# A gradient along rows: tiles of 256 adjoining rows, or two of each partition's 64 rows

## The chip, the cores and the metric

The kernel runs on one core of one Trainium2 chip. The metric is device time in microseconds (us) of one execution, as the median of several runs; lower is better. A profile is one more execution, recorded by the hardware profiler, with a time of its own.

## The reference

```python
def setup_inputs():
    return {"x": np.random.randn(8192, 8192).astype(np.float32)}

def reference(x):
    return np.gradient(x, axis=1)
```

Along each row, an inner column gets half the difference of its two neighbours, (x[j+1] - x[j-1]) / 2. The first column gets x[1] - x[0] and the last one x[8191] - x[8190], both without the half. The matrix has 256 MiB, which are read once and written once: 536.87 MB (with 1 MB = 10^6 bytes).

## The kernel before

**Tiles.** A row has m = 8192 elements of 4 bytes, 32 KB. A tile takes R = 2 rows on each of the 128 partitions, so 256 rows, and there are nsets = 32 tiles. In the kernel before, tile s is the rows 256 s to 256 s + 255, and partition p holds the rows 256 s + 2 p and 256 s + 2 p + 1 of it: a piece of 64 KB that lies without a gap in DRAM, right behind the piece of partition p - 1. A tile is thus one run of 8.39 MB in DRAM. The output is cut in the same way.

**Buffers.** Three slots (NB = 3) of 64 + 16384 elements a partition rotate. A tile is loaded into the elements from 64 on, and its result is written from element 0 on, in the same slot. A small tile `ends` keeps four edge values a partition for each tile.

**One tile's work** (the loop over i):

- L52, on SyncE's DMA queue (SP): the load of the tile, one DMA of 8.39 MB.
- L74, on GpSimd (POOL): one small subtraction takes both rows' first and last differences into `ends`. It waits for the load.
- L80, on VectorE (DVE): one custom operation over both rows at once, 128 x 16382 elements, writes half the difference of the neighbours. It waits for L74, since it writes over what L74 reads.
- L91, on VectorE, or for some tiles on GpSimd: a copy of the four edge values to their places in the result. It waits for L80.
- L56, on SP: the store of the tile, one DMA of 8.39 MB. It waits for L91.

**The order of the transfers.** All loads and stores are issued by SP, in an order written out by hand: the loads of tiles 0, 1 and 2; then the tiles' stores as they get ready; behind the store of every third tile, the next three loads. A load waits until the store that used its slot three tiles before has landed. The store of a tile with i % 3 = 1 is held back until the next tile has landed (the variable `held`). So transfers go by threes: three loads, three stores, three loads, and so on.

The lines that decide where a tile lies in DRAM are L27 and L28; every load reads `x_sets[i]` and every store writes `out_sets[i]`.

Of the kernel before, what the change touches and what calls it, by code (L numbers as in the profile page):

```python
# [1 line left out]

# [4 lines left out]


@with_exitstack
def kernel(  # L10
    ctx: ExitStack,
    tc: tile.TileContext,
    x: bass.AP,
    out: bass.AP,
):

    nc = tc.nc
    P = nc.NUM_PARTITIONS
    n, m = x.shape
    R = 2  # L20
    NB = 3
    SH = 64
    W = R * m
    nsets = n // (P * R)
    f32 = x.dtype

    x_sets = x.rearrange("(s p t) m -> s p (t m)", p=P, t=R)  # L27
    out_sets = out.rearrange("(s p t) m -> s p (t m)", p=P, t=R)  # L28

    pool = ctx.enter_context(tc.tile_pool(name="pool", bufs=1))  # L30
    edge = 256 // 4
    nends = nsets * R * 2
    ends_pad = pool.tile([P, nends + edge // 2], f32, name="ends", tag="ends")
    ends = ends_pad[:, 0:nends].rearrange("p (s t e) -> p s t e", t=R, e=2)
    slots = [pool.tile([P, SH + W], f32, name=f"slot{k}", tag=f"slot{k}") for k in range(NB)]
    loads, stores = [], [None] * nsets
    in_front = {}

    def chain(i, ins, *needed):

        group, engine = f"slot{i % NB}", ins.ins.engine
        keep = [o.ins for o in needed]
        if in_front.get(engine, (None,))[0] == group:
            keep.append(in_front[engine][1])
        tc.declare_no_dep(ins.ins, group=group, keep=keep, reason="implied by the needed step")
        tc.add_to_no_dep_group(group, ins.ins)
        in_front[engine] = group, ins.ins
        return ins

    def load(i):  # L50
        b = slots[i % NB]
        ins = nc.sync.dma_start(out=b[:, SH : SH + W], in_=x_sets[i])  # L52
        loads.append(chain(i, ins, *([stores[i - NB]] if i >= NB else [])))

    def store(i, done, later):
        ins = nc.sync.dma_start(out=out_sets[i], in_=slots[i % NB][:, 0:W])  # L56
        stores[i] = chain(i, ins, done)
        if later is not None:
            tc.add_manual_dep(
                ins.ins,  # L60
                later.ins.name,
                mybir.DependencyInfo(mybir.DependencyClass.Sync, mybir.DependencyReason.DATA),
                reason="issued once the next tile has landed",
            )

    held = None
    with tc.manual_schedule():
        for i in range(NB):
            load(i)
        for i in range(nsets):  # L70
            b = slots[i % NB]
            xin = b[:, SH : SH + W].rearrange("p (t m) -> p t m", m=m)

            ins = nc.gpsimd.tensor_sub(  # L74
                out=ends[:, i, :, :],
                in0=xin[:, :, 1 : m : m - 2],
                in1=xin[:, :, 0 : m - 1 : m - 2],
            )
            at = [chain(i, ins, loads[i])]
            ins = nc.vector._custom_dve(  # L80
                dve_ops.TENSOR_TENSOR_REDUCE_SUB_MAX,
                out=b[:, 1 : W - 1],
                in0=b[:, SH + 2 : SH + W],
                in1=b[:, SH : SH + W - 2],
                s0=0.0,
                s1=0.5,
            )
            halved = chain(i, ins, *at)
            res = b[:, 0:W].rearrange("p (t m) -> p t m", m=m)
            placer = nc.gpsimd if i % 5 in (1, 3) and i < nsets - 2 else nc.vector  # L90
            ins = placer.tensor_copy(out=res[:, :, 0 : m : m - 1], in_=ends[:, i, :, :])  # L91
            placed = chain(i, ins, halved)
            if held is not None:
                store(*held, at[0])
                held = None
            if i % NB == 1 and i + 1 < nsets:
                held = i, placed
            else:
                store(i, placed, None)
            if i % NB == NB - 1:  # L100
                for k in range(i + 1, min(i + 1 + NB, nsets)):
                    load(k)


# [1 line left out]
_INS = ['x']  # L106
_OUTS = [((8192, 8192), 'float32')]


# [23 lines left out]
```

## Time and profile before

| | us |
|---|---|
| median of 3 runs | 1247.27 (1246.84 to 1247.35) |
| the profiled execution | 1246.62 |
| its span, from the first to the last instruction | 1244.7 |
| 32 L80 operations on VectorE, 17.22 each | 551.2 |
| 32 L74 operations on GpSimd, 0.198 each | 6.3 |
| 32 L91 copies, 20 on VectorE and 12 on GpSimd | 5.7 |
| issue to landing of a load, median | 57.9 |
| issue to landing of a store, median | 40.2 |

The page gives each engine's busy time, then the span in 40 equal slices of some 31 us, in which a digit is the busy share in tenths; the rows DMA and GB/s of the slices show how busy the core's 16 DMA engines were and what they moved, reads and writes together. Below that, DMA queues are listed with their packets (pieces that one DMA engine moves as one) and bytes, and groups of instructions with their count, busy time, the mean time of one in ns, and the idle time of their engine before them with what ended it. The trace also has a record of each DMA packet with its size, start and duration; it does not say which engine or partition a packet belongs to. The time from issue to landing counts the wait behind earlier transfers too. TensorE and ScalarE are not used.

### The profile page before, as it was taken

How to read it: one execution, taken by the hardware profiler on the slowest of the kernel's cores; microseconds unless marked ns; L12 is line 12 of the kernel's file. 1: busy time of each engine (PE TensorE's matmuls, PEld its weight loads, DVE VectorE, ACT ScalarE, POOL GpSimd, SP SyncE). 2: the span in 40 equal slices, each digit the busy share in tenths (PEclk: the TensorE clock that was granted, in tenths of full speed). 3: DMA queues.
4: the chain of work that ended last, by engine and by line, in shares of the span. 5: the costliest groups of instructions: out<-in, count | busy, mean ns of one | idle time of the engine just before them, and what ended most of it. 6: DMA issues, size and time to landing. Idle time of an engine off the chain costs nothing.

```text
span 1244.7 us, 237 instructions
## 1 busy us (share of the span) xinstructions
DVE 554.6 (45%) x52; POOL 8.8 (1%) x48
## 2 busy tenths in 40 slices
DVE  2850582079009702850582079009603840591082
POOL 0000000000000000000000000000000000000000
DMA  9999999999999999999999999999999999999999
GB/s 404 438 436 423 421 438 438 438 438 428 432 430 430 438 438 438 423 436 436 430 434 436 438 428 432 438 436 434 425 436 434 432 436 436 436 434 430 434 409 404
DMA packets 9217, 536.88 MB, mean 431 GB/s; under 512 B 1024, under 2 KB 1024, under 8 KB 1024
## 3 DMA queue, kind: packets, MB, share of 16 engines
q1 hardware_dynamic: 9216, 536.88, 99.8%
q14 instruction: 1, 0.01, 0.0%
HBM read 268.44 MB, written 268.44 MB: 431 GB/s over the span
## 4 chain that ended last, share of the span: by engine, by line
another core or an unknown queue 74%; DVE 18%; DMA 3%; issue 2%; POOL 1%; SPq 0%; POOLq 0%
DVE slot L80 18%; DMA slot<-in_x_dram 3%; POOL ends L74 0%; POOL slot L91 0%; SPq L52 0%; POOLq L128 0%; DVE slot L91 0%
## 5 line engine op out<-in xcount | busy, mean ns | idle before, releaser
L80 DVE CUSTOM_DVE_ANT_0 slot<-slot 128x16382 f32<-128x16382 f32 x32 | 551.2, 17224 | 667.6 <-POOL ends L74 667.6
L74 POOL TENSOR_TENSOR ends<-slot 128x4 f32<-128x4 f32 x32 | 6.3, 198 | 988.5 <-DMA slot<-in_x_dram 988.5
L91 POOL COPY slot<-ends 128x4 f32<-128x4 f32 x12 | 2.3, 190 | 207.9 <-DVE slot L80 207.9
L91 DVE COPY slot<-ends 128x4 f32<-128x4 f32 x20 | 3.4, 172 | 0.7
L117 POOL MEMSET const-bfloat16-1.0<- 128x1 bf16 x1 | 0.1, 101 | 0.0
L117 POOL MEMSET const-uint8-127<- 128x1 uint8 x1 | 0.1, 101 | 0.0
L117 POOL MEMSET const-float32-0.0<- 128x1 f32 x1 | 0.1, 98 | 0.2 <-issue 0.2
L117 POOL MEMSET const-float32-1.0<- 128x1 f32 x1 | 0.1, 98 | 0.0
## 6 DMA issues: line engine op xcount, KB each, us to landing
slot<-in_x_dram SPq DMA_DIRECT2D x32, 57.9
out_dram<-slot SPq DMA_DIRECT2D x32, 40.2
```

The costliest lines, as they stand in the source:

```text
L74: ins = nc.gpsimd.tensor_sub(out=ends[:, i, :, :], in0=xin[:, :, 1 : m : m - 2], in1=xin[:, :, 0 : m - 1 : m - 2],)
L80: ins = nc.vector._custom_dve(dve_ops.TENSOR_TENSOR_REDUCE_SUB_MAX, out=b[:, 1 : W - 1], in0=b[:, SH + 2 : SH + W], in1=b[:, SH : SH + W - 2],
L91: ins = placer.tensor_copy(out=res[:, :, 0 : m : m - 1], in_=ends[:, i, :, :])
L117: nc = _bacc.Bacc("TRN2", target_bir_lowering=False, num_devices=1)
```

## The change

Each partition owns 64 adjoining rows of the matrix (64 p to 64 p + 63, 2 MiB), and tile s takes the rows 64 p + 2 s and 64 p + 2 s + 1 of every partition p. A partition's piece of a tile is still 64 KB without a gap. The piece of the next partition lies 2 MiB further on, in the input and in the output, and the next tile's piece of the same partition right behind this one's. Nothing else is edited; each engine issues the same instructions in the same order.

```diff
-    x_sets = x.rearrange("(s p t) m -> s p (t m)", p=P, t=R)
-    out_sets = out.rearrange("(s p t) m -> s p (t m)", p=P, t=R)
+    x_sets = x.rearrange("(p s t) m -> s p (t m)", s=nsets, t=R)
+    out_sets = out.rearrange("(p s t) m -> s p (t m)", s=nsets, t=R)
```

## The prediction

> **What bounds the kernel now.** First the page's busy time and its slices.
>
> ```profile
> span 1244.7 us, 237 instructions
> ...
> DVE 554.6 (45%) x52; POOL 8.8 (1%) x48
> ...
> DVE  2850582079009702850582079009603840591082
> ...
> DMA  9999999999999999999999999999999999999999
> GB/s 404 438 436 423 421 438 438 438 438 428 432 430 430 438 438 438 423 436 436 430 434 436 438 428 432 438 436 434 425 436 434 432 436 436 436 434 430 434 409 404
> DMA packets 9217, 536.88 MB, mean 431 GB/s; under 512 B 1024, under 2 KB 1024, under 8 KB 1024
> ...
> q1 hardware_dynamic: 9216, 536.88, 99.8%
> ```
>
> The reader is to see that VectorE idles for whole slices (digit 0) while the DMA row is 9 in every slice: the 16 DMA engines are busy for 99.8% of the span, and nothing else comes near. Of the 9,216 packets of q1, 1,024 are under 512 B (64 transfers x 16 engines, the completion marks) and 8,192 carry 64 KB: one packet for each partition's piece of a tile (2 rows x 8192 x 4 B), 128 in a transfer, 8 per engine.
>
> Next the waits, to see whether an engine ever holds a transfer up.
>
> ```profile
> POOL ends L74 <- DMA slot<-in_x_dram: 988.5, 32, 77.4
> DVE slot L80 <- POOL ends L74: 667.6, 32, 60.2
> POOL slot L91 <- DVE slot L80: 207.9, 12, 17.3
> ```
>
> All three end at the first one: compute waits for landings. The chain of waits gives 74% to "another core or an unknown queue"; there is one core, and in the timeline those pieces are the stretches in which only transfers run.
>
> Last, two windows in which the engines only store (77.6 to 116.4; in the packet records stores 0 to 2 run from 61 to 119) and two in which they only load (135.8 to 174.6).
>
> ```profile
> 77.60:97.00 19.40, 2.40 (x2) 0.00 (x0) 1.00 1.00 432
> 97.00:116.40 19.40, 0.00 (x0) 0.00 (x0) 1.00 1.00 432
> ...
> 135.80:155.20 19.40, 15.23 (x1) 0.20 (x1) 1.00 1.00 432
> 155.20:174.60 19.40, 17.32 (x2) 0.39 (x2) 1.00 1.00 432
> ```
>
> The last column is GB/s. Reading alone and writing alone run at the same 432, with VectorE idle or busy. The trace's packet records say why this looks like a limit of the DMA engines and not of HBM: the median 64 KB packet takes 2.418 us, the shortest 2.415, load or store (27.1 GB/s per engine, x16 = 434). So the floor is 8192 / 16 = 512 packets per engine x 2.418 = 1238.0 us. 170 packets are longer than 2.45 us, 52.9 us too long together, 3.3 us per engine; start, end and completion marks make up the rest of 1244.7. HBM answers fast enough for the DMA engines here; how much it has to spare the trace does not show.
>
> **The change, part by part.** (1) Both edited lines change DRAM addresses only. A partition's piece of a tile is still 64 KB without a gap, so there are still 64 transfers, 8,192 packets of 64 KB and 1,024 marks. Each engine's list of instructions is the same in number and order, SP's included; nothing is moved past a queue and no wait is added. VectorE (32 x 17.22 us), GpSimd and the issues (0.34 us each) cost the same: 0 us. If transfers get longer this work is covered better: a store's compute, 17.22 + 0.2 + 0.2 us, lies beside two later transfers of 8 x 2.418 = 19.3 us each.
>
> (2) What changes is the distance between the places in HBM that the 16 engines touch at one time. Before, neighbouring partitions' pieces are 64 KB apart and a tile is one run of 8.4 MB. After, they are 64 rows x 32 KB = 2 MiB apart, and a tile is 128 runs of 64 KB over all 256 MiB, in x and in out alike. Engines that work on different partitions then work at addresses whose lower 21 bits differ only by how far one is ahead of another within its piece. The records show how little that is: in the stores and loads from 61 to 235 us the first 16 packets of a transfer start within 0.57 us, a quarter of a packet, some 15 KB; by the end of the kernel that has grown to 2.15 us and falls back to 0.39 us in the last two transfers. So the 16 streams walk nearly in step. If HBM serves addresses that share their lower bits from few of its parts, all 16 streams meet there, all the time.
>
> No packet of before runs in that pattern, so its price is bounded from both sides. Below: a packet keeps 2.418 us and the sum is 0. It can't fall by much, since 2.415 is the shortest of 8,192: at most 512 x 0.003 = 1.5 us, and the 3.3 us of long packets. Above: the longest packet is 3.536 us, + 1.118 x 512 = 572 us. Between lie two rows: the mean of the 170 long packets, 2.729 us (+ 0.311 x 512 = 159), and the 14 long packets of the very first transfer, when all engines ask a cold memory at once, 3.043 us in the mean (+ 0.625 x 512 = 320). I take the last, because it is the only place in the trace where HBM visibly keeps all 16 engines waiting together; it is an estimate by likeness, since part of its 0.6 us is the latency of a first access and would not recur in a full pipeline.
>
> The Trainium skill has a rule on this in "DMA: Bandwidth & Descriptors", section "Latency and other measured facts": copies of 128-partition tiles between HBM tensors ran at full rate (214 GB/s each way) with a padded pitch, at 207 with 512 KiB between partitions, 164 with 2 MiB and 103 with 4 MiB; its reason, streams in step falling on the same channels, it calls an inference. The trace agrees with its full rate (431 / 2 = 215.5 each way) and cannot show the rest. By its ratio at 2 MiB the sum would be 1246.6 x 214 / 164 = 1627 us, where mine is 1566.
>
> **Sum.** The profiled execution took 1246.62 us (span 1244.7 and 1.9 around it). 1246.6 + 320 = 1566 us; the median of the runs shown, 1247.27, lies 0.65 above the profiled one, so 1567 us, 26% slower, at about 343 GB/s.
>
> **Rivals.** *No difference* (same): the engines, at 2.418 us a packet, are the limit and HBM has enough to spare. For it: the unvarying 2.418 in loads and stores alike, and that streams which start multiples of 64 KB apart, also a power of two, run at full speed already. An engine that is held up also falls behind the others, and the step is lost: the spread did grow to 2.15 us. Against it: 2 MiB takes away five more address bits in which engines can differ. 1247 us. The Trainium skill speaks for it in "HBM Reference", "Specifications (TRN2)": about 716 GB/s for a domain, and a lone core bounded by its DMA engines; the 431 measured here is 60% of that, and no run here shows the rest.
>
> *Not slower, and faster*: 129 of the 170 long packets lie in the third load of a group of three (51 in the first such load, then up to 16 in one); if these are collisions of neighbouring places, which pieces 2 MiB apart would not have, the 3.3 us go, and 1247.3 - 3.3 = 1244 us. This decides only if regular packets keep their 2.418.
>
> *One direction only*: loads or stores alone are slowed, since groups of three transfers of one kind alternate. Half the packets at 3.043: 256 x 0.625 = 160, so 1407 us. For it: 157 of the 170 long packets are loads. Against it: both tensors get the same pitch, and both directions ran at the same 432.
>
> *Dearer*: the meeting place is narrower than a cold start, and every packet is like the longest: 1247 + 572 = 1819 us or more. For it: nothing but that row; against it: engines that wait for each other drift apart.
>
> **Chances.** Slowed in both directions, forecast 1567: 0.62, with its own range 1406 (every packet like the mean long one) to 1714 (every packet like the mean of the 20 longest, 3.33 us: + 0.912 x 512 = 467). One direction, 1407: 0.13. Dearer, 1819: 0.10. No difference, 1247: 0.12. Faster, 1244: 0.03. The range runs from 1245, so that it takes in no difference, to 1714; left out are faster, dearer and a small tail of the forecast, some 0.15 together. A measurement of this kernel tells about 0.2% (2.5 us) from no change. Faster by more than that 0.03, within it 0.12, slower 0.85.
>
> **What the profile after would show.** If right: the same 8,192 packets and the same instruction counts, 17.22 us for the VectorE operation, DMA still busy in every slice, about 343 GB/s in all slices, and packets of about 3.04 us in loads and stores; the wait of L74 for landings grows by about the whole 320 us, since nothing else gets longer. If only one direction suffers, GB/s alternates between about 432 and 345 in groups of three transfers. If nothing happens, 2.418 us stays the median. I am wrong in kind if the median packet stays at 2.418 but gaps appear between packets, or if packets split or their number changes; wrong in size if the median packet is far from 3.04.

## The result, and the profile after

| | before | after |
|---|---|---|
| median, us | 1247.28 (1246.84 to 1247.52) | 1311.06 (1305.34 to 1317.47) |
| profiled execution / its span, us | 1246.62 / 1244.7 | 1308.73 / 1306.8 |
| 64 KB packets, median / mean, us | 2.418 / 2.425 | 2.418 / 2.530 |
| packets over 2.45 us | 170 of 8,192 | 1,838 of 8,192 |

After takes 1.0517 times as long as before (95% interval 1.0495 to 1.0539): 5.2% or 64 us slower, where 26% and 320 us were forecast. The page of the kernel after:

```profile
span 1306.8 us, 237 instructions
...
DVE 554.6 (42%) x52; POOL 8.9 (1%) x48
...
DVE  1850185048206800950383069009604830780190
...
DMA  9999999999999999999999999999999999999988
GB/s 353 417 397 375 385 433 433 369 431 433 429 369 437 427 439 387 425 433 397 429 421 437 395 429 437 427 405 437 427 413 423 438 431 409 433 423 423 423 305 291
DMA packets 9217, 536.88 MB, mean 411 GB/s; under 512 B 1024, under 2 KB 1024, under 8 KB 1024
...
q1 hardware_dynamic: 9216, 536.88, 99.2%
```

Instructions, VectorE's 554.6 us and the packets' number and sizes are as before. The DMA row is still 9, but for the last two slices, so the share of busy time shows next to nothing: a packet that takes longer counts as busy. The loss is in the GB/s row, and it isn't even: 353 to 417 in the first five slices, then 433 again with a dip, to 369 at first, to 387 to 405 midway and to some 410 later, in every fourth slice or so (about 120 us apart, one group of three loads and three stores), and 305 and 291 at the end. The waits:

```profile
POOL ends L74 <- DMA slot<-in_x_dram: 1039.6, 32, 87.6
DVE slot L80 <- POOL ends L74: 718.8, 32, 70.4
POOL slot L91 <- DVE slot L80: 207.9, 12, 17.3
```

L74 waits 51.1 us longer for landings; the rest of the 62.1 us of span lies behind the last landing, in the last two stores. Nothing waits for anything new. Windows cut at the first packet of a group of six transfers give the loss by place (last column GB/s). Before, the first two groups and the last four transfers:

```profile
1.80:119.40 117.60, 52.01 (x5) 0.79 (x4) 1.00 0.99 425
119.40:235.30 115.90, 52.02 (x5) 0.78 (x4) 1.00 1.00 434
...
1163.50:1243.50 80.00, 34.79 (x4) 0.40 (x2) 1.00 0.97 419
```

And after:

```profile
1.80:130.40 128.60, 52.01 (x5) 0.79 (x4) 1.00 1.02 391
130.40:252.50 122.10, 52.01 (x5) 0.79 (x4) 1.00 1.00 412
...
1208.20:1305.10 96.90, 34.79 (x4) 0.40 (x2) 1.00 0.91 346
```

The first group lost 11.0 us, groups two to ten together 33.7 (6.2 in the second, 2.3 in the tenth), the last four transfers 16.9. With 0.5 for start and marks that is the whole 62.1. Long packets carry most of it: summed over all packets, the time above 2.418 us is 57.5 us per engine, 3.4 before; the other 8.0 us are idle engines, by the queue's share above (99.2% against 99.8%).

Around one turn after (store 3 starts at 192, load 6 at 253, store 6 at 313), windows of 19.4 us:

```profile
213.40:232.80 19.40, 0.00 (x0) 0.00 (x0) 1.00 1.01 432
232.80:252.20 19.40, 0.00 (x0) 0.00 (x0) 1.00 1.04 388
252.20:271.60 19.40, 0.00 (x0) 0.00 (x0) 1.00 0.96 368
271.60:291.00 19.40, 12.46 (x1) 0.20 (x1) 1.00 1.00 432
```

The dip is where the last store of a group meets the first load of the next, the turn. Beside it both loads and stores run at the old 432, although every piece lies 2 MiB from its neighbour. The packet records say how: in the second group's last two loads, 154 to 195 us, the 16 engines' packets start spread over 2.34 us of the 2.42 that a packet takes, and all 256 take 2.418; in the first load they started within 1.4 us and took 2.81 in the mean. In the last two stores they start within 0.40 and 1.1 us, and take 3.03 and 3.05. The engines got out of step by themselves, and in these two loads the new layout costs nothing. A wide spread alone doesn't ensure that: store 1, in the first group, starts spread over 2.57 us, and all its 128 packets are long, 2.60 us in the mean. What makes the difference these traces don't show.

### The profile page after: what moved, and what is told of

Its sections match the earlier page's. It is cut to its first block, busy times and chain, and to the rows that moved or that the text cites. A ratio compares the mean times of both kernels' runs of the same rounds, so it can differ in the third digit from the quotient of the medians.

```text
span 1306.8 us, 237 instructions
## 1 busy us (share of the span) xinstructions
DVE 554.6 (42%) x52; POOL 8.9 (1%) x48
## 3 DMA queue, kind: packets, MB, share of 16 engines
q1 hardware_dynamic: 9216, 536.88, 99.2%
## 4 chain that ended last, share of the span: by engine, by line
another core or an unknown queue 74%; DVE 17%; DMA 4%; issue 2%; POOL 1%; SPq 0%; POOLq 0%
DVE slot L80 17%; DMA slot<-in_x_dram 4%; POOL ends L74 0%; POOL slot L91 0%; SPq L52 0%; POOLq L128 0%; DVE slot L91 0%
## 5 line engine op out<-in xcount | busy, mean ns | idle before, releaser
L74 POOL TENSOR_TENSOR ends<-slot 128x4 f32<-128x4 f32 x32 | 6.4, 200 | 1039.6 <-DMA slot<-in_x_dram 1039.6
```

The lines of the kernel that those rows point to most:

```text
L74: ins = nc.gpsimd.tensor_sub(out=ends[:, i, :, :], in0=xin[:, :, 1 : m : m - 2], in1=xin[:, :, 0 : m - 1 : m - 2],)
```

## The experiments

The edits are shown shortened where a note or "..." says so. Theory *in-step*: streams that walk in step at places alike in their lower address bits collide; the collisions push them apart, and then the cost ends. Rival *far-places*: pieces far apart cost by themselves, at first visits and at every change between input and output. Later rivals stand with their runs.

**Another distance, just as far.** 62 rows to a partition; the last 256 rows are one tile as before.

```diff
-    x_sets = x.rearrange("(p s t) m -> s p (t m)", s=nsets, t=R)
-    out_sets = out.rearrange("(p s t) m -> s p (t m)", s=nsets, t=R)
+    x_sets, out_sets = cut(x), cut(out)   # rows 0:7936 as "(p s t) m" with s=31, rows 7936:8192 as "(p t) m" (shortened)
```

> Partitions own 62 adjoining rows, so pieces lie 2 MiB less 64 KB apart (tiles 0 to 30); the last 256 rows are one tile as in the kernel before. Theory in-step (streams walking in step at addresses alike in their lower 21 bits collide until they drift apart): the lower bits now differ, so about 1247 us (1243 to 1252), packets 2.418 us, no cluster of long packets. Theory far-places (what costs is that neighbouring pieces lie some 2 MiB apart, at the first visit and at every turn between input and output): unchanged, about 1311 us (1300 to 1320).

1246.32 us, 0.9993 of before (0.9984 to 1.0003).

```profile
span 1244.6 us, 237 instructions
...
GB/s 404 438 436 428 419 436 438 438 438 436 436 428 425 432 438 438 436 438 434 430 430 425 438 438 430 436 434 434 428 434 436 438 436 434 432 434 432 432 404 404
```

No dip is left, and groups two to ten take 115.9 to 116.2 us each, as before. Distance and the number of separate places are as after, so far-places falls: what costs is the round 2 MiB.

**One slot instead of three.** Each transfer then starts alone, on idle DMA engines.

```diff
-    NB = 3
+    NB = 1
...
```

For the layout after, and for that before (one execution each; the part left out only guards the held store):

> The kernel after with one slot instead of three, so each transfer starts on idle DMA engines, all 16 together, with nothing beside it; the time is some 32 x (2 x 20 + 18 + waits), about 2000 us, and only the packets are of interest. In-step: all 64 transfers are slow, 2.8 to 3.1 us a packet, loads and stores alike, from the first to the last. Far-places or cold first visits: long packets only at the start of each transfer, most 2.418 us. Turns (reads beside writes): no long packets at all, since reads and writes never overlap.

> The kernel before with one slot, the control for the one-slot run of the kernel after. In-step: starting together costs nothing when neighbouring pieces are 64 KB apart, so stores take 2.42 to 2.45 us a packet and last 19.4 to 19.7 us each (after: 3.04 and 24.9), loads 2.42 to 2.5; about 32 x (5.4 + 4.3) = 310 us less than after's 2234, so 1900 to 1960 us. If starting together is itself what costs (a burst on a cold memory, whatever the addresses): stores near 3.0 us here too.

2234.45 and 1933.42 us. The stores (tile out_dram) with the layout after, then with that of before:

```profile
DMA to landing us min/median/max: 26.4/26.7/27.4
```

```profile
DMA to landing us min/median/max: 20.7/20.7/21.7
```

No store of one overlaps the range of the other: 6 us on each, from the first to the last. Inside three stores after, and three before:

```profile
46.50:68.50 22.00, 0.00 (x0) 0.00 (x0) 1.00 0.99 334
116.50:138.50 22.00, 0.00 (x0) 0.00 (x0) 1.00 1.00 334
186.50:208.50 22.00, 0.00 (x0) 0.00 (x0) 1.00 1.00 334
```

```profile
42.00:60.00 18.00, 0.00 (x0) 0.00 (x0) 1.00 0.94 408
103.00:120.00 17.00, 0.00 (x0) 0.00 (x0) 1.00 1.00 432
163.00:180.00 17.00, 0.00 (x0) 0.00 (x0) 1.00 1.00 432
```

334 GB/s against 432, with the same packets: 3.039 us in the mean against 2.422. Loads took 2.80 (2.70 to 2.93 by load, at its lowest a little under in-step's 2.8) against 2.50. The 2.50 is above 2.42 because some 16 packets at the start of each load (12 to 23) are long, the longest 3.3 to 3.6 us, even with the layout before. There the first 16 packets of a load take 3.08 us in the mean and the others 2.419; stores, which start from idle too, don't show it. Started together each time, the new layout costs 301 us in 64 transfers, close to the 320 of the forecast; with three slots most transfers don't start together.

**The same stores, not started together.** One slot, layout after, and ahead of each store:

```diff
+        for j, k in enumerate((13, 10, 7, 4)):
+            small = nc.sync.dma_start(
+                out=ahead[0:k, j * 4096 : (j + 1) * 4096],
+                in_=x[0 : 2 * k, :].rearrange("(p t) m -> p (t m)", t=2)[:, 0:4096],
+            )
+            tc.add_manual_dep(small.ins, done.ins.name, ...)
...
```

> One slot and the layout after; four small extra loads ahead of each store (13, 10, 7 and 4 rows of 16 KB, one row to an engine, into a tile that nobody reads) give the engines 0 to 4 x 0.6 us of other work first, so that they start the store in five groups instead of all together. They move 34 x 16 KB more per tile, some 2.5 us. In-step: the stores, 3.04 us a packet when started together, fall clearly, to 2.42 to 2.75 us, with the same addresses in the same order. Far-places, or a store path that is slow at this pitch whatever the timing: they stay at 2.95 to 3.1.

The stores' packets fell from 3.039 to 2.529 us in the mean. Their first 16 starts are spread over 3.7 to 4.5 us, where they had lain within 0.15. Inside three stores, while all engines are at work:

```profile
53.00:66.00 13.00, 0.00 (x0) 0.00 (x0) 1.00 1.03 423
127.00:140.00 13.00, 0.00 (x0) 0.00 (x0) 1.00 1.01 413
201.00:214.00 13.00, 0.00 (x0) 0.00 (x0) 1.00 1.02 418
```

That is 413 to 423 GB/s where it was 334. Same addresses, same order, another timing: the step is the cause. Spreading saves no time this way: the run as a whole, 2374.26 us (one execution), is longer. The small packets took 0.6 to 2.4 us, 2.2 in the median, and not 0.6, and from its first start to its last end a store took 27.5 us against 24.9.

**Loads or stores alone.** One of the two rearranged lines taken back:

```diff
-    out_sets = out.rearrange("(p s t) m -> s p (t m)", s=nsets, t=R)
+    out_sets = out.rearrange("(s p t) m -> s p (t m)", p=P, t=R)
```

> Loads as in the kernel after (2 MiB between partitions), stores as in the kernel before; the rows of the result land in another order. In-step: the first loads are as slow as after, stores never; the turns from stores to loads cost less, since the two sides no longer share their lower bits: 1255 to 1285 us. Far-places: about half the loss, 1279 us, at the turns to the input only. A theory that only stores suffer: 1247 us.

1265.97 us, 1.0150 of before (1.0133 to 1.0167): within in-step's numbers, outside the others'. And with `x_sets` taken back instead:

> Loads as in the kernel before, stores as in the kernel after; the rows of the result land in another order. In-step: long packets in the first stores and in the last two transfers (some 10 us there), 1260 to 1285 us. Far-places: about half the loss, 1279 us. A theory that only loads suffer: 1247 us.

1318.20 us, 1.0559 (1.0524 to 1.0594). No theory had this, in-step (1260 to 1285) included: stores alone cost about what stores and loads cost together (1.0517, 1.0495 to 1.0539). Whether they cost more isn't shown, since the two intervals overlap.

```profile
GB/s 412 412 347 327 369 420 375 371 377 430 401 367 428 432 426 393 432 432 428 395 438 430 405 434 432 434 410 436 430 412 430 432 425 407 434 432 410 432 317 286
```

The loss is early, 347 to 327 in the first stores and again 375 to 377 in the second group's. Loads that don't collide leave the engines in step (in this run the first 16 packets of the second and of the third load start within 0.56 us), so the first stores start in step and take 3.0 to 3.1 us a packet in the first two, the second group's first two 2.8 to 2.9, the third's 2.6 to 2.7. Groups one to three lose 19.8, 14.5 and 8.4 us against the floor of 116.1, in the kernel after 12.6, 6.0 and 5.4. There the loads collide too, fall apart fast, and hand a spread to the stores, whose first two take 2.55 to 2.60 us: this is how we read the two traces, no run tried it by itself. The range of the starts isn't the whole measure: in this run the second group's first store starts spread over 2.0 us and still collides, but 15 of its 16 engines start within 1.1 us.

**Shorter round distances.** The matrix in two halves, 1 MiB apart, or four quarters, 512 KiB apart:

```diff
-    x_sets = x.rearrange("(p s t) m -> s p (t m)", s=nsets, t=R)
-    out_sets = out.rearrange("(p s t) m -> s p (t m)", s=nsets, t=R)
+    x_sets, out_sets = cut(x), cut(out)   # "(h p s t) m -> h s p (t m)", s = 16 or 8, tile i is [i // s, i % s] (shortened)
```

> 1 MiB between partitions: each owns 32 rows of one half of the matrix, first half first. In-step: one more lower bit in which engines can differ, so a part of the loss of 64 us: 1260 to 1295 us. Far-places: little less than after, 1295 to 1315.

> 512 KiB between partitions: each owns 16 rows of one quarter of the matrix. In-step: two more lower bits, loss nearly gone, 1245 to 1262 us. Far-places: 1280 to 1310.

1294.42 us (1.0385, 1.0369 to 1.0401) and 1264.59 us (1.0136, 1.0119 to 1.0153). The cost falls with each halving, though 512 KiB still costs 2.6 us more than in-step was given; far-places is out for 512 KiB, while 1294 lies in in-step's range and just below that of far-places.

**Three times as many turns.** Stores and loads alternate one by one:

```diff
-            if i % NB == 1 and i + 1 < nsets:
-                held = i, placed
-            else:
-                store(i, placed, None)
-            if i % NB == NB - 1:
-                for k in range(i + 1, min(i + 1 + NB, nsets)):
-                    load(k)
+            store(i, placed, None)
+            if 0 < i <= nsets - NB:
+                load(i + NB - 1)
```

> The kernel before with another order of the transfers: after the first loads, stores and loads alternate one by one (each load is issued behind the next tile's store), so the engines turn from writing to reading some 29 times instead of 10. Control: with pieces 64 KB apart a turn costs nothing in the trace of before, so 1243 to 1256 us. If every turn costs something by itself: above 1260.

> The kernel after in the same alternating order. Theory turns (in the kernel after, groups two to ten of six transfers each last 2.2 to 6.0 us more than 116.1, 3.7 in the mean, and the long packets sit where the last store meets the first load): about 29 x 3.7 = 107 us for the turns, some 12 for the start and some 19 for the end, 1350 to 1420 us. In-step alone (turns cost only because groups of one kind let the streams lock; mixing reads and writes keeps them out of step): 1311 us or less, 1270 to 1312.

Before's layout 1247.52 us (1.0004, 0.9995 to 1.0014), after's 1364.85 us (1.0951, 1.0923 to 1.0978), inside the range of the theory of turns, though its sum (107 + 12 + 19 = 138 us more than before) is 21 us too high. After, alternating:

```profile
GB/s 368 409 416 343 360 389 411 376 376 393 397 401 374 380 405 409 407 393 391 412 424 407 399 389 416 426 403 395 407 416 424 397 397 409 422 426 387 403 355 278
```

The dips have spread over the whole span. Turns cost, and only with the round distance.

**What collides at a turn.** Output moved within each partition's 2 MiB, by 16 (shown), 8, 24 and 4 tiles:

```diff
-        ins = nc.sync.dma_start(out=out_sets[i], in_=slots[i % NB][:, 0:W])
+        ins = nc.sync.dma_start(out=out_sets[(i + nsets // 2) % nsets], in_=slots[i % NB][:, 0:W])
```

> The kernel after, but each store goes 1 MiB further on in its partition's 2 MiB (half way round), so what is written and what is read at one time differ in one more lower bit; reads among themselves and writes among themselves are as in the kernel after. The rows of the result land in another order. Theory cross (at a turn, one engine's reads collide with another's writes because input and output are alike in their lower bits): the 33 us of the turns fall by half or more, 1275 to 1297 us. Theory own side (each side collides with itself when the turn upsets the drift): no change, 1303 to 1320 us.

> As the run with stores turned by half, but by a quarter: each store goes 512 KiB further on in its partition's 2 MiB. The rows of the result land in another order. The half turn made the kernel slower (1344 us), against both theories' numbers. Cross (reads and writes of different engines collide, by how far apart input and output lie in their lower bits): the loss of groups two to ten, 33 us unturned and 67 at a half, changes with the turn, and among a quarter, three quarters and an eighth one lies clearly below 33: total at most 1298 us. Own side: all three give about 1311 us.

> Each store goes 1.5 MiB further on (three quarters round); the rows of the result land in another order. Cross: another value than the quarter, see there, between 1280 and 1360 us. Own side: about 1311 us.

> Each store goes 256 KiB further on (an eighth round); the rows of the result land in another order. Cross: near the unturned kernel if the lower bits that matter lie above 256 KiB, 1295 to 1325 us, else another value. Own side: about 1311 us.

| output moved by | us | ratio (95%) | groups 2 to 10 above 116.06 each, us in all |
|---|---|---|---|
| 0 (the kernel after) | 1311.06 | 1.0517 (1.0495 to 1.0539) | 33 |
| an eighth | 1329.47 | 1.0663 (1.0628 to 1.0699) | 50 |
| a quarter | 1330.64 | 1.0679 (1.0661 to 1.0697) | 44 |
| half | 1343.64 | 1.0766 (1.0742 to 1.0790) | 67 |
| three quarters | 1328.12 | 1.0651 (1.0632 to 1.0670) | 41 |

Neither theory's numbers came, but for three quarters round, which lies in *cross*'s wide range without differing from the quarter. *Own side* falls as it was put, since the distance between input and output does matter. *Cross* fails as it was put, since no distance tried makes a turn cheap. The earlier runs say more. In the kernel after, packets at turns four to ten (a group's last store and the next group's first load) are too long by 2.6 us a turn and engine. With only the stores apart it is 2.3, 1.7 of it in the store; with only the loads apart 0.6, all in the load. So a turn costs without both sides having the round distance, and most of it comes with the stores. Which accesses meet at a turn stays open. The moved output also made the first group (14.7 to 16.6 us, 12.5 unmoved) and the last four transfers dearer, which this account doesn't explain. Nothing tried beats before: the 62-row layout equals it.

## Why the prediction was wrong

The direction was right, the size five times too big (64 us, not 320). The measured 1311 us lies below the forecast's own range, 1406 to 1714; the range given, from 1245 on, held it only because it was drawn down to take in no difference, and that is luck.

- *What bounds the kernel*: right. The DMA engines are the limit at 2.418 us a packet; that median is the same after. (Of the 170 long packets, 131 and not 129 lie in third loads, in order of their starts; nothing hangs on it.)
- *Nothing but DRAM addresses moves*: right. Instruction counts, packets and VectorE's time didn't change.
- *Streams in step at a round distance collide*: right, shown by the 62-row run (no loss at about the same distance), the one-slot pair (334 against 432 GB/s) and the spread stores (3.04 to 2.53 us).
- *The price, 3.043 us*: right for stores in step (3.039), too much for loads (2.80), and for a reason that does not hold. The row it came from, the cold start, is no collision: with the layout before and one slot, the first 16 packets of a load from idle take 3.08 us in the mean, and the rest 2.419. That the two numbers agree is chance.
- *"So the 16 streams walk nearly in step"*, and meet *"all the time"*: this is the step that failed. The term + 0.625 x 512 = 320 us gave the price to all 512 packets of each engine; 1,838 of 8,192 are long at all, the median stays at 2.418 and not near 3.04, and long packets add 54.1 us per engine (57.5 against 3.4). The step of before was measured in a kernel in which little disturbs it: there the spread of the starts grew slowly, from 0.57 us at 235 us to 2.2 at 893. In the kernel after they are spread over 2.70 us by the first store, at 66 us. The text had this mechanism among the reasons for *no difference* ("an engine that is held up also falls behind the others, and the step is lost") and took it as a case of its own, where it is what ends the forecast's own case early. What then remains is the start (11.0 us), the end (16.9) and groups two to ten, nearly all of it at the turns (33.7).
- *The end*, which no term of the sum had: engines out of step finish a load at different times, store 30 has to wait for the slowest one's piece of load 30, and the early engines run dry (DMA share 0.72 from 1241 to 1267 us). So they start store 30 within 0.40 us of each other (0.42 in the kernel before, where it costs nothing), and the last two stores take 24.8 and 25.8 us, like the one-slot stores' 24.9.
- *The turns*: not foreseen. In groups two to ten the packets' excess is 32.7 us per engine, 15.3 in last stores and 14.2 in first loads. That turns cost is shown by their number too (29 instead of 10: 1364.85 us); why is open.
- *One direction only*: wrong as a rival. Loads alone cost 1.5% and stores alone 5.6%, which don't add up to the 5.2% of both. Our reading, which no run tried by itself, is that each side sets the step in which the other starts.

The Trainium skill's rule ("DMA: Bandwidth & Descriptors", "Latency and other measured facts"), 164 of 214 GB/s at 2 MiB, a ratio of 0.766, agrees with stores in step (334 / 432 = 0.773) and not with this kernel (411 / 431 = 0.954); at 512 KiB it has 207 / 214 = 0.967, and here the time ratio of 1.0136 makes 0.987. Its inference of streams in step at the same place agrees with the spread stores. Its remedy, a pitch of 4 MiB padded by 4 KiB, at which it has the full 214, agrees in kind with the 62-row run.

## What to carry to other kernels

Pieces 512 KiB to 2 MiB (a power of two) apart cost here where the DMA engines are in step and at changes from stores to loads. So price them for the stretches in which engines start together (the first transfers, each transfer that starts on a dry queue, the last ones) and for each such change, not for every packet. A distance that is not round, here 2 MiB less 64 KB, takes the whole cost away. Read such a change in GB/s by window and in packet durations; the busy share of DMA hardly shows it (99.2% against 99.8%).

## What the runs showed of the hardware that was not expected

Colliding loads drift apart within a group or so (first load 2.81 us a packet, the second group's last two 2.42), while colliding stores do so more slowly: with loads that don't collide, the second group's first two stores were still at 2.8 to 2.9 us a packet. So giving both tensors the round distance (5.2%) cost no more, within the noise, than giving it to the output alone (5.6%). And at the turn at 250 us the last 16 packets of a store took 3.6 to 4.8 us and the first of a load up to 4.4, on engines whose starts were spread over 2.4 us, where with the layout before both took 2.42 to 2.44.
